# Turning the cross-attention softmax weights on VectorE and through DRAM in a hybrid trunk step

## The chip, the cores and the metric

The kernel runs on one core of a Trainium2 chip. The metric is the time of one execution on the device in microseconds (us); lower is better. PE is TensorE, DVE is VectorE, ACT is ScalarE, POOL is GpSimd and SP is SyncE, whose queue issues most loads. All arithmetic is in float32; matmuls that need the full precision are done in three passes on operands that are split into a high and a low part.

## What is computed

One step of a decoder layer for a prompt group (1024 tokens) and a sample group (8 sequences, one token each). One projection of the normalised input feeds three branches: gated linear attention (GLA), multi-scale causal pooling, and cross-attention into 256 memory tokens (4 heads, head dimension 256). The three are gated, summed and projected out. The change touches the cross-attention of the prompt group:

```python
def cross_attn(q, mk, mv):
    """q: (B,T,H,Dh); mk, mv: (B,M,H,Dh)."""
    s = jnp.einsum('bthd,bmhd->bhtm', q.astype(jnp.float32), mk.astype(jnp.float32)) * (XA_HEAD_DIM ** -0.5)
    p = jax.nn.softmax(s, axis=-1)
    o = jnp.einsum('bhtm,bmhd->bthd', p, mv.astype(jnp.float32))
    return o.astype(q.dtype)

def mixer_layer(...):
    h = rmsnorm(x, norm_gain)
    proj = h @ w_in
    q, k, v, gla_g, a_lr, u, pool_g, xq, xg, merge = jnp.split(proj, split_pts, axis=-1)
    ...
    c = cross_attn(xq.reshape(B, T, XA_HEADS, XA_HEAD_DIM), mem_k, mem_v).reshape(B, T, XA_WIDTH)
    br_x = c * jax.nn.silu(xg)
    branches = jnp.stack([br_gla, br_pool, br_x], axis=2)
    bproj = jnp.einsum('btnw,nwd->btnd', branches, w_branch)
    ...
```

The softmax's weights p have tokens on the partitions (rows); the product with the values contracts over memory tokens, so it needs them with memory tokens on the partitions. The turning between the two is what the change is about.

## The kernel before

**Products.** The input projection is cut into pairs of 128 output columns. Each pair is computed by seven products of a fast block scheme, each product in two halves of 12 matmuls into a PSUM buffer named px (six of these). ACT and DVE read px (names r and c) and hand it on. The weights come by SP into `raw`; DVE and ACT make sums (`ws`) and high and low parts (`a11h`, `s2l` and so on), three products ahead of their use. These products keep PE busy for most of the kernel's first two thirds.

**Work put between.** After each half of a product, `fill` takes more work from a generator, in units of cost that each `yield` states, so that it is spread evenly over the products. First comes `cross_steps`, then the GLA. The matmuls of this work use two more PSUM buffers, named pz.

**The cross stage.** `cross_steps` walks over 16 steps s, one for each head h = s // 4 and each chunk c of 256 tokens. Step s does, in this order: `cross_scores` of s (matmuls, then the maximum nm on DVE, exp into the tile p on ACT, a reciprocal and two scalings on DVE), the split of the queries of s + 1 (`xqsh`, `xq`), the load of the queries of s + 2, once a head the load of the memory's keys and values (`mkv`), then `cross_values` of s - 2 and `cross_weights` of s - 1. `cross_weights` turns p by four transposes on PE (L716) into pz and splits the result into `pTh` (ACT, L222) and `pTl` (DVE, L223). `cross_values` contracts these with the values `mvsh` and `mkv` in 12 matmuls (`mm3`, L241 to L243), ACT copies the result to `xo` (L728), and POOL stores it (`mixsc`, L729). Between these stands the sample group's attention, `cross_sample`: its keys `kc` and its queries `qb` come by SP, DVE multiplies and sums them (L769), PE turns and contracts them (`sc`, `ps`, `pm`, `vc`, L783 to L819). The sample queries reach `qb` by way of a store by POOL (`xqs`, L744).

**Queues.** The orders of PE and SP are those in which the program is written. The order on ACT, DVE and POOL is set by a scheduler when the program is built. A queue runs in order: an instruction that waits holds what stands behind it.

**Buffers.** Most tiles of 128x512 in this stage come from one ring of NR = 14 SBUF buffers (`R`): queries, p, the turned weights, xo, the split keys and values. A new tile takes a buffer whose last tile is done with, and its first writer waits for the last reader of that one. `kc`, `qb` and `vc` come from four buffers of their own (`V`).

Two helpers on which the change rests: `split_in` splits a tile that lies in SBUF, the low part written over the source, and `loaded` takes a ring buffer and issues a load on SP.

Of the kernel before, what the change touches and what calls it, by code (L numbers as in the profile page):

```python
# [18 lines left out]
P = 128  # L19
# [5 lines left out]
NH = 4  # L25
# [8 lines left out]
CT = 256  # L34
# [13 lines left out]
def trunk_kernel(ctx: ExitStack, tc: tile.TileContext,  # L48
# [3 lines left out]
    nc = tc.nc  # L52
# [46 lines left out]
    def PZ():  # L99
        return ps.tile([P, 512], F32, tag="pz", name="pz", bufs=2)  # L100
# [13 lines left out]
    def R(shape, dt=F32, name="r"):  # L114

        return shaped(wk.tile([P, 512], dt, tag="ring", name=name, bufs=NR), shape)
# [20 lines left out]
    ident = cp.tile([P, P], F32, name="ident")  # L137
# [63 lines left out]
    def scratch(n, name, shape):  # L201
        return [dr.tile(list(shape), F32, name=f"{name}{i}") for i in range(n)]

    PAIR = (P, 4, HT)
    xq_scr, v_scr = scratch(NH, "xqs", (NS, 256)), scratch(NH, "vs", (NS, 256))
    acc_scr = [scratch(NK, f"acc{n}_", (P, TT)) for n in range(2)]
    mkv_scr = [scratch(NH, f"mkvs{o}", (P, 2, DV)) for o in range(2)]
    al_scr = scratch(2, "als", (P, HT))
# [19 lines left out]
    def split_r(src, shape, name, scale=None):  # L228
        hi, lo = R(shape, F32R, name + "h"), R(shape, F32R, name + "l")
        split(hi, lo, src, scale)  # L230
        return hi, lo
# [440 lines left out]
    cross = {}  # L672

    def cross_load(h):
        cross["raw", h] = [loaded(mkv_scr[o][h], [2, DV], "mkv") for o in range(2)]
# [16 lines left out]
    def cross_scores(h, c):  # L692
        xh, xl = cross["q", h, c]
        mh, ml = cross["mk", h]
        t = PZ()
        for j in range(2):
            for i in range(2):
                cs = slice(j * P, (j + 1) * P)
                mm3(t[:, j * NM:(j + 1) * NM], xh[:, i, cs], xl[:, i, cs], mh[:, i], ml[:, i], i == 0, i == 1)
        nm = tiny(2, "nm")  # L700
        nc.vector.tensor_reduce(nm, t.rearrange("p (j m) -> p j m", j=2), axis=AX.X, op=ALU.max, negate=True)
        p = R([2, NM], name="p")
        sm = tiny(2, "sm")
        for j in range(2):
            act(p[:, j], t[:, j * NM:(j + 1) * NM], AF.Exp, bias=nm[:, j:j + 1], accum_out=sm[:, j:j + 1])
        nc.vector.reciprocal(sm, sm)
        for j in range(2):
            nc.vector.tensor_scalar(p[:, j], p[:, j], sm[:, j:j + 1], None, op0=ALU.mult)
        cross["p", h, c] = p

    def cross_weights(h, c):
        p = cross["p", h, c]
        t = PZ()
        for a in range(2):
            for j in range(2):
                nc.tensor.transpose(t[:, (2 * a + j) * P:(2 * a + j + 1) * P], p[:, j, a * P:(a + 1) * P], ident)  # L716
        cross["pT", h, c] = split_r(t.rearrange("p (a t) -> p a t", a=2), [2, CT], "pT")

    def cross_values(h, c):
        ph, pl_ = cross["pT", h, c]  # L720
        vh, vl = cross["mv", h]
        g = R([2, CT], name="xo")
        t = PZ()
        for i in range(2):
            cs = slice(i * P, (i + 1) * P)
            for a in range(2):
                mm3(t[:, i * CT:(i + 1) * CT], vh[:, a, cs], vl[:, a, cs], ph[:, a], pl_[:, a], a == 0, a == 1)
        nc.scalar.activation(g, t.rearrange("p (i t) -> p i t", i=2), AF.Copy)  # L728
        nc.gpsimd.dma_start(out=mix_chunk(2, h, c), in_=g)  # L729

# [93 lines left out]
    def cross_steps():  # L824
        def scores(n):
            cross_scores(n // 4, n % 4)

        def memory(n):
            if n % 4 == 0:
                cross_memory(n // 4)  # L830

        def weights(n):
            cross_weights(n // 4, n % 4)

        def values(n):
            cross_values(n // 4, n % 4)

        samples = chain_of(cross_sample(h) for h in range(NH))
        cross_load(0)
        cross_memory(0)  # L840
        cross_fetch(0, 0)
        yield 2
        cross_queries(0, 0)
        cross_fetch(0, 1)
        for s in range(16 + 2):
            if s < 16:
                scores(s)
                yield 3
                if s + 1 < 16:
                    cross_queries(*divmod(s + 1, 4))  # L850
                if s + 2 < 16:
                    cross_fetch(*divmod(s + 2, 4))
            if s % 4 == 2 and s < 14:
                cross_load(s // 4 + 1)
            if s >= 1:
                yield next(samples, 0)
            if 0 <= s - 2:
                values(s - 2)
                yield 1.7
            if s >= 1:  # L860
                yield next(samples, 0)
            if s % 4 == 3 and s < 15:
                memory(s + 1)
                yield 2
            if 0 <= s - 1 < 16:
                weights(s - 1)
                yield 1.7
            for _ in range(3):
                if s >= 1:
                    yield next(samples, 0)  # L870
        yield from samples
# [689 lines left out]
```

## Time and profile before

| | |
|---|---|
| median of 3 runs | 1450.72 us (1450.0 to 1452.0) |
| the profiled execution | 1452.08 us, span of the instructions 1450.2 us |
| granted TensorE clock | 0.999 |
| PE busy | 1421.7 us, 98% of the span |
| DVE, ACT, POOL busy | 906.0, 689.2, 194.9 us (62%, 48%, 13%) |
| traffic | 259.42 MB, mean 179 GB/s |
| the cross stage's steps | softmax of the first step at 125.4 us, of the last at 337.5 us |

A profile is of one execution. "L716" is line 716 of the kernel. A group of instructions is written as line, engine, operation, output <- inputs, count, then busy time, mean time of one in ns, and the idle time of the engine ahead of them with what ended it. A row of waits gives what was waited for, the sum in us, how often, and the longest. The chain that ended last is the path of work followed back from the last instruction. A row with three times such as 569/597/600 gives the shortest, the middle and the longest in ns.

### The profile page before, as it was taken

To read this page: it belongs to the slowest core of one execution; us is meant where nothing else is said; L and a number is where in the kernel's file an instruction comes from. 1 tells how busy PE (TensorE), PEld (TensorE's weight loads), DVE (VectorE), ACT (ScalarE), POOL (GpSimd) and SP (SyncE) were. 2 spreads that over 40 slices of the span, in tenths; PEclk is the share of its full clock that TensorE was granted. 3 is DMA by queue.
4 is the path that set the end of the run, shared out by engine and by line. 5 is a ranking of instruction groups with operands and counts; after the bars stand their busy time and mean duration, and the time that the engine had idled before them with its cause. 6 is when DMAs were issued, how large, how long until landed. Compare 5 with 4: busy or idle time off the path is not lost.

```text
span 1450.2 us, 28260 instructions
## 1 busy us (share of the span) xinstructions
PE 1421.7 (98%) x10753; PEld 1360.2 (94%) x10753; DVE 906.0 (62%) x2107; ACT 689.2 (48%) x1607; POOL 194.9 (13%) x353
## 2 busy tenths in 40 slices
PE   7999999998999999999999999999999999999998
PEld 6899999998899999999999999999999999999876
DVE  6956656666686767766756678785672434544436
ACT  6744435443465666656654445454472333233312
POOL 3112101124341111111111111110010000000000
PEclk9999999999999999999999999999999999999999
DMA  9346665666655453553544455455594677632633
GB/s 335 122 159 207 200 212 184 218 190 164 160 157 183 130 182 126 177 175 125 180 142 152 157 187 182 138 192 168 194 303 147 226 255 236 241 116 71 220 125 117
DMA packets 182739, 259.42 MB, mean 179 GB/s; under 512 B 21436, under 2 KB 131796, under 8 KB 182596
## 3 DMA queue, kind: packets, MB, share of 16 engines
q1 hardware_dynamic: 159900, 183.87, 41.4%
q0 software_dynamic: 22560, 73.56, 14.1%
q8 instruction: 84, 1.38, 0.4%
q14 instruction: 51, 0.42, 0.1%
q10 hardware_dynamic: 144, 0.20, 0.0%
HBM read 180.47 MB, written 77.56 MB: 178 GB/s over the span
## 4 chain that ended last, share of the span: by engine, by line
PE 86%; DMA 5%; DVE 5%; issue 2%; ACT 1%; SPq 0%; DVEq 0%; POOL 0%; ACTq 0%
PE px L241 25%; PE px L242 24%; PE px L243 24%; DMA qb<-xqs 2%; PE pz L243 2%; PE pz L242 2%; PE pz L241 2%; DMA raw<-in_w_in_dram 2%; DVE kc L769 1%; PE pz L403 1%; PE pz L955 1%; PE pz L936 1%; PE pz L809 1%; PE pz L938 1%; DVE ws L304 0%
## 5 line engine op out<-in xcount | busy, mean ns | idle before, releaser
L243 PE MATMUL px<-bh,wbl 128*128 128x384 f32 (+1 forms) x576 | 184.1, 320 | 0.0
L242 PE MATMUL px<-bl,wbh 128*128 128x384 f32 (+1 forms) x576 | 184.1, 320 | 0.0
L241 PE MATMUL px<-bh,wbh 128*128 128x384 f32 (+1 forms) x576 | 183.7, 319 | 0.0
L553 ACT ACTIVATE r<-px 128x258 f32<-128x258 f32 x240 | 90.0, 376 | 45.6 <-PE px L243 45.0
L241 PEld LDWEIGHTS px<-bh,wbh 128*128 128x128 f32 x576 | 108.3, 188 | 0.0
L242 PEld LDWEIGHTS px<-bl,wbh 128*128 128x128 f32 x576 | 108.2, 188 | 0.0
L243 PEld LDWEIGHTS px<-bh,wbl 128*128 128x128 f32 x576 | 108.2, 188 | 0.0
L241 PE MATMUL px<-ot,s1h 128*128 128x258 f32 x320 | 93.9, 293 | 0.0
L241 PE MATMUL px<-ot,s3h 128*128 128x258 f32 x320 | 93.4, 292 | 0.0
L241 PE MATMUL px<-o,s4h 128*128 128x258 f32 x320 | 93.2, 291 | 0.2 <-DVE c L628 0.2
L241 PE MATMUL px<-o,a11h 128*128 128x258 f32 x320 | 92.9, 290 | 0.0
L241 PE MATMUL px<-o,a12h 128*128 128x258 f32 x320 | 92.9, 290 | 0.0
L241 PE MATMUL px<-ot,a22h 128*128 128x258 f32 x320 | 92.9, 290 | 0.0
L241 PE MATMUL px<-ot,s2h 128*128 128x258 f32 x320 | 92.3, 288 | 0.0
L242 PE MATMUL px<-o,a11h 128*128 128x258 f32 x320 | 91.0, 284 | 0.3 <-DVE o L223 0.3
L243 PE MATMUL px<-o,a11l 128*128 128x258 f32 x320 | 90.6, 283 | 0.0
L242 PE MATMUL px<-ot,a22h 128*128 128x258 f32 x320 | 90.5, 283 | 0.0
L242 PE MATMUL px<-ot,s2h 128*128 128x258 f32 x320 | 90.0, 281 | 0.5 <-DVE ot L223 0.5
L243 PE MATMUL px<-ot,s3l 128*128 128x258 f32 x320 | 90.5, 283 | 0.0
L243 PE MATMUL px<-o,a12l 128*128 128x258 f32 x320 | 90.4, 283 | 0.0
L242 PE MATMUL px<-o,a12h 128*128 128x258 f32 x320 | 90.4, 283 | 0.0
L243 PE MATMUL px<-ot,s1l 128*128 128x258 f32 x320 | 90.4, 282 | 0.0
(470 smaller groups left out, 4616.0 us busy)
## 6 DMA issues: line engine op xcount, KB each, us to landing
raw<-in_w_in_dram SPq DMA_DIRECT2D x80, 512.0 KB, 4.0
msc<-c POOLq DMA_DIRECT2D x24, 516.0 KB, 4.3
brsc<-c POOLq DMA_DIRECT2D x24, 516.0 KB, 4.0
sig<-msc SPq DMA_DIRECT2D x24, 516.0 KB, 6.6
mix<-mixsc SPq DMA_DIRECT2D x48, 256.0 KB, 4.5
brr<-brsc SPq DMA_DIRECT2D x48, 256.0 KB, 5.2
wbr<-in_w_branch_dram SPq DMA_DIRECT2D x24, 512.0 KB, 6.1
acc<-sig POOLq DMA_DIRECT2D x16, 516.0 KB, 5.3
```

The costliest lines, as they stand in the source:

```text
L241: nc.tensor.matmul(out, lhsT=lh, rhs=rh, start=start, stop=False, skip_group_check=more)
L242: nc.tensor.matmul(out, lhsT=lh, rhs=rl, start=False, stop=False, skip_group_check=more)
L243: nc.tensor.matmul(out, lhsT=ll, rhs=rh, start=False, stop=stop, skip_group_check=more)
L403: nc.tensor.matmul(t[:, :DV], lhsT=memT[k // 2][:, k % 2, a * P:(a + 1) * P], rhs=raw[k // 2][:, k % 2], start=k == 0, stop=k == NK - 1)
L553: nc.scalar.activation(r, acc[c][:, :QT], AF.Copy)
L769: nc.vector.tensor_tensor_reduce(kc[:, a, :], kc[:, a, :], qb[:, bb, :], scale=1.0, scalar=0.0, op0=ALU.mult, op1=ALU.add, accum_out=sc[:, ...
L809: nc.tensor.matmul(t[32 * j:32 * j + 32, :DV], lhsT=pm[:, a, 4 * i + j, :], rhs=vc[j][:, a, :], start=a == 0, stop=a == 1)
L936: nc.tensor.matmul(t[0:64, 0:P], lhsT=ki[:, 0:64], rhs=qi, start=True, stop=True)
L938: nc.tensor.transpose(t[:, P:2 * P], kt, ident)
L955: nc.tensor.matmul(to, lhsT=kiqi[:, 1, cs], rhs=st, start=False, stop=True)
```

## The change

After the softmax, DVE turns each 32x32 block of p (`STREAM_TRANSPOSE`) into a new tile pt. POOL stores pt to a DRAM scratch in four DMAs, one for each 32 partitions, in pieces of 64 elements. Two steps later SP loads it back into a tile pT with memory tokens on the partitions (`cross_turned`). `cross_weights` splits pT where it lies, and `cross_values` reads the parts in runs of 32 elements, since the columns lie in another order. The weights of a step are split in the iteration two after its softmax (one after it before), and the values are computed in the third (the second before), so the loop has one iteration more. The four PE transposes of each step are gone. Everything else of the program is as it was; lines behind L206 move by one, so that L241 is L242 after, and further by five behind `cross_values`.

```diff
     PAIR = (P, 4, HT)
     xq_scr, v_scr = scratch(NH, "xqs", (NS, 256)), scratch(NH, "vs", (NS, 256))
+    pt_scr = scratch(4 * NH, "pts", (8, 32, 4, 64))
     acc_scr = [scratch(NK, f"acc{n}_", (P, TT)) for n in range(2)]
     mkv_scr = [scratch(NH, f"mkvs{o}", (P, 2, DV)) for o in range(2)]
     al_scr = scratch(2, "als", (P, HT))
@@ -706,15 +707,17 @@
         nc.vector.reciprocal(sm, sm)
         for j in range(2):
             nc.vector.tensor_scalar(p[:, j], p[:, j], sm[:, j:j + 1], None, op0=ALU.mult)
-        cross["p", h, c] = p
+        pt = R([512], name="pt")
+        nc.vector.transpose(pt.rearrange("p (b j c) -> p j b c", j=2, c=32), p.rearrange("p j (b c) -> p j b c", c=32))
+        for q in range(4):
+            nc.gpsimd.dma_start(out=pt_scr[4 * h + c][:, :, q, :].rearrange("b r x -> r b x"),
+                                in_=pt[32 * q:32 * q + 32].rearrange("r (b x) -> r b x", b=8))
 
     def cross_weights(h, c):
-        p = cross["p", h, c]
-        t = PZ()
-        for a in range(2):
-            for j in range(2):
-                nc.tensor.transpose(t[:, (2 * a + j) * P:(2 * a + j + 1) * P], p[:, j, a * P:(a + 1) * P], ident)
-        cross["pT", h, c] = split_r(t.rearrange("p (a t) -> p a t", a=2), [2, CT], "pT")
+        cross["pT", h, c] = split_in(cross["pr", h, c], [2, CT], "pT")
+
+    def cross_turned(h, c):
+        cross["pr", h, c] = loaded(pt_scr[4 * h + c].rearrange("(a b) r q x -> (b r) a (q x)", a=2), [2, CT], "pT")
 
     def cross_values(h, c):
         ph, pl_ = cross["pT", h, c]
@@ -724,7 +727,9 @@
         for i in range(2):
             cs = slice(i * P, (i + 1) * P)
             for a in range(2):
-                mm3(t[:, i * CT:(i + 1) * CT], vh[:, a, cs], vl[:, a, cs], ph[:, a], pl_[:, a], a == 0, a == 1)
+                rh, rl = (x[:, a].rearrange("p (q j c) -> p j q c", q=4, j=2) for x in (ph, pl_))
+                mm3(t[:, i * CT:(i + 1) * CT].rearrange("p (j q c) -> p j q c", j=2, q=4), vh[:, a, cs], vl[:, a, cs],
+                    rh, rl, a == 0, a == 1)
         nc.scalar.activation(g, t.rearrange("p (i t) -> p i t", i=2), AF.Copy)
         nc.gpsimd.dma_start(out=mix_chunk(2, h, c), in_=g)
 
@@ -842,7 +847,7 @@
         yield 2
         cross_queries(0, 0)
         cross_fetch(0, 1)
-        for s in range(16 + 2):
+        for s in range(16 + 3):
             if s < 16:
                 scores(s)
                 yield 3
@@ -852,18 +857,20 @@
                     cross_fetch(*divmod(s + 2, 4))
             if s % 4 == 2 and s < 14:
                 cross_load(s // 4 + 1)
+            if 0 <= s - 2 < 16:
+                cross_turned(*divmod(s - 2, 4))
             if s >= 1:
                 yield next(samples, 0)
-            if 0 <= s - 2:
-                values(s - 2)
+            if 0 <= s - 3:
+                values(s - 3)
                 yield 1.7
             if s >= 1:
                 yield next(samples, 0)
             if s % 4 == 3 and s < 15:
                 memory(s + 1)
                 yield 2
-            if 0 <= s - 1 < 16:
-                weights(s - 1)
+            if 0 <= s - 2 < 16:
+                weights(s - 2)
                 yield 1.7
             for _ in range(3):
                 if s >= 1:
```

By the counts of the program, 64 transposes on PE are left out, and 16 DVE transposes, 64 issues on POOL and 16 loads on SP are added.

**PE, first step whose weights are turned.** Matmuls of a product (px, from the operands ot and s1h) stand around the four transposes; before:

```order
646 L241 MATMUL px<-ot_756,s1h 128x258
647 L242 MATMUL px<-ot_757,s1h 128x258
648 L243 MATMUL px<-ot_756,s1l 128x258
649 L716 MATMUL pz<-ident,p 128x128 x4
650 L241 MATMUL px<-ot_752,s1h 128x258
651 L242 MATMUL px<-ot_753,s1h 128x258
```

After:

```order
646 L242 MATMUL px<-ot_772,s1h 128x258
647 L243 MATMUL px<-ot_773,s1h 128x258
648 L244 MATMUL px<-ot_772,s1l 128x258
649 L242 MATMUL px<-ot_768,s1h 128x258
650 L243 MATMUL px<-ot_769,s1h 128x258
651 L244 MATMUL px<-ot_768,s1l 128x258
```

The transposes are gone and the matmuls of the product follow each other.

**SP, step s = 6** (third step of the second head). The queries (xq), the next head's keys and values (mkv), then the sample group's keys (kc) and queries (qb); raw are weights of the projection. In brackets stand the semaphores that an issue waits on. Before:

```order
89 L662 DMA xq<-xqsc_172 128x2x256 [waits DMASW3_49,DMASW1_49,PE_49]
90 L662 DMA mkv<-mkvs_150 128x512 [waits DMASW7_49,PE_49]
91 L662 DMA mkv<-mkvs_154 128x512 [waits DMAHW3_49,PE_49]
92 L662 DMA kc<-in_cache_mem_k_dram 128x2x256 [waits DMAHW4_49]
93 L662 DMA kc<-in_cache_mem_k_dram 128x2x256 [waits DMAHW6_49,DMAHW5_49,DVE_49]
94 L759 DMA qb<-xqs_125 128x512 [waits DMAHW0_49,DVE_49]
95 L295 DMA raw<-in_w_in_dram 128x4x256 [waits DMAHW7_49,DVE_49]
96 L662 DMA kc<-in_cache_mem_k_dram 128x2x256
97 L662 DMA kc<-in_cache_mem_k_dram 128x2x256 [waits DMAHW4_49,DMAHW1_49,DVE_49]
98 L759 DMA qb<-xqs_125 128x512 [waits DMAHW5_49,DMAHW2_49,DVE_49]
```

After:

```order
93 L663 DMA xq<-xqsc_188 128x2x256 [waits DMAHW5_49,DMASW5_49,PE_49]
94 L663 DMA mkv<-mkvs_166 128x512 [waits DMAHW6_49,PE_49]
95 L663 DMA mkv<-mkvs_170 128x512 [waits DMASW5_49,DMASW6_49,DMASW4_49,DMASW7_49,DMASW3_49,DMAHW7_49,DMASW2_49,DVE_49]
96 L663 DMA pT<-pts_136 128x2x256 [waits DMAHW0_49,PE_49]
97 L663 DMA kc<-in_cache_mem_k_dram 128x2x256 [waits DMAHW1_49]
98 L663 DMA kc<-in_cache_mem_k_dram 128x2x256 [waits DMAHW2_49,DVE_49]
99 L764 DMA qb<-xqs_125 128x512 [waits DMAHW4_49,DMAHW3_49,DVE_49]
100 L663 DMA kc<-in_cache_mem_k_dram 128x2x256
101 L663 DMA kc<-in_cache_mem_k_dram 128x2x256 [waits DMAHW5_49,DMAHW1_49,DVE_49]
102 L764 DMA qb<-xqs_125 128x512 [waits DMAHW6_49,DMAHW2_49,DVE_49]
103 L296 DMA raw<-in_w_in_dram 128x4x256 [waits DMAHW7_49]
```

The load of the turned weights (pT) has come between mkv and kc, and waits on PE. The load of raw stands behind the second qb of these rows and no longer between the two.

**POOL, beginning of the cross stage.** The xqsc and mixsc rows store products and mixed values, smp is a small copy, xqs are the sample group's queries. Before:

```order
66 L587 DMA xqsc_171<-c_1175 128x2x516
67 L568 COPY smp<-c_1427 128x8
68 L587 DMA xqsc_171<-c_1427 128x1032
69 L744 DMA xqs_124<-qn 8x256
70 L568 COPY smp<-c_1541 128x2x4
71 L587 DMA xqsc_172<-c_1541 128x2x516
72 L729 DMA mixsc_0_182<-xo 256x1x256
```

After:

```order
66 L588 DMA xqsc_187<-c_1191 128x2x516
67 L569 COPY smp<-c_1443 128x8
68 L588 DMA xqsc_187<-c_1443 128x1032
69 L713 DMA pts_132<-pt 32x8x64 x4
70 L713 DMA pts_133<-pt 32x8x64 x4
71 L749 DMA xqs_124<-qn 8x256
72 L713 DMA pts_134<-pt 32x8x64 x4
73 L569 COPY smp<-c_1563 128x2x4
74 L588 DMA xqsc_188<-c_1563 128x2x516
```

The stores of the first two steps' turned weights stand ahead of xqs, those of the third behind it.

**ACT, step s = 6.** The copy of the values (xo), the high part of the turned weights (pTh), and the releases of px (r, c) and high parts of weights around them. Before:

```order
186 L728 ACTIVATE xo<-pz 128x512
187 L647 ACTIVATE c_2598<-px 128x258
188 L222 ACTIVATE s3h<-ws 128x512
189 L647 ACTIVATE c_2598<-px 128x258
190 L222 ACTIVATE pTh<-pz 128x512
191 L222 ACTIVATE a11h<-raw 128x512
```

After:

```order
182 L733 ACTIVATE xo<-pz 128x512
183 L223 ACTIVATE s2h<-ws 128x512
184 L554 ACTIVATE r_2632<-px 128x258
185 L223 ACTIVATE pTh<-pT 128x512
186 L223 ACTIVATE s1h<-ws 128x512
187 L648 ACTIVATE c_2652<-px 128x258
```

The split of the weights now reads SBUF (pT) where it read PSUM (pz); it stands three rows behind the copy of the values where it stood four behind it.

## The prediction

> **What bounds the kernel now.** I read the page first (busy time and the chain that ended last), then busy time by stretch, where 100 to 340 us holds the 16 steps of the cross stage, 340 to 380 us its last sample work, and 380 to 1300 us what follows.
>
> ```profile
> PE 1421.7 (98%) x10753; PEld 1360.2 (94%) x10753; DVE 906.0 (62%) x2107; ACT 689.2 (48%) x1607; POOL 194.9 (13%) x353
> PE 86%; DMA 5%; DVE 5%; issue 2%; ACT 1%; SPq 0%; DVEq 0%; POOL 0%; ACTq 0%
> 100.00:340.00 240.00, 236.31 (x1983) 229.15 (x1982) 152.87 (x386) 108.14 (x262) 40.47 (x73) 1.00 0.62 191
> 340.00:380.00 40.00, 32.72 (x272) 29.56 (x271) 18.42 (x50) 12.00 (x27) 16.46 (x27) 1.00 0.68 196
> 380.00:1300.00 920.00, 917.47 (x7160) 899.51 (x7160) 592.57 (x1397) 469.21 (x1118) 111.48 (x186) 1.00 0.55 177
> ```
>
> The columns of the last three rows are length, then PE, PE's weight loads, DVE, ACT and POOL, the granted clock, the share of the DMA engines and GB/s. PE is the bound: from 380 to 1300 us it stands still for 920.00 − 917.47 = 2.5 us. Whatever PE gains before 380 us is therefore carried to the end, since little is there for a shift to fall into. In the two earlier stretches PE stands still for 3.7 and 7.3 us, 11.0 together, and the waits of PE from 100 to 380 us say for what:
>
> ```profile
> PE pz L795 <- DVE ps L790: 2.7, 1, 2.7
> PE pz L242 <- DVE pTl L223: 1.8, 1, 1.8
> PE pz L809 <- DMA vc<-in_cache_mem_v_dram: 1.7, 1, 1.7
> PE pz L241 <- ACT xqsh L225: 1.4, 1, 1.4
> PE pz L243 <- DVE xq L226: 1.3, 2, 1.0
> PE pz L716 <- ACT xo L728: 1.1, 1, 1.1
> PE pz L241 <- DVE pTl L223: 0.8, 1, 0.8
> PE pz L783 <- DVE mkTl L223: 0.2, 1, 0.2
> ```
>
> Three of them hang on the turned weights: 1.8, 1.1 and 0.8, or 3.7 us. So the change can win by PE work that goes, and by these waits, and it can lose by any new wait of PE.
>
> **What goes from PE.** Each of the 16 steps drops four transposes on the identity. Here is the first group in the timeline of PE, then the chain at that group and at a late one, then all groups by line:
>
> ```profile
> 134.44 0.28 PE L243 MATMUL px<-ot,s1l 128*128 128x258 f32 x1
> 134.56 0.60 PE L716 MATMUL pz<-ident,p 128*128 128x128 f32 x4
> 134.92 0.37 PE L241 MATMUL px<-ot,s1h 128*128 128x258 f32 x1
> 135.12 0.28 PE L242 MATMUL px<-ot,s1h 128*128 128x258 f32 x1
> ```
> ```profile
> 134.73 0.44 PE pz L716 x4
> ...
> 316.11 0.44 PE pz L716 x4
> ```
> ```profile
> L716 PE MATMUL pz<-ident,p 128*128 128x128 f32 x64 | 9.7, 273 | 1.1 <-ACT xo L728 1.1
> ```
>
> Matmuls of a product start 0.12 us apart (134.44 to 134.56). From the start of the last one before the group to the start of the second after it are 135.12 − 134.44 = 0.68 us; two of the ordinary distance are 0.24, so the group costs 0.44 us. The chain says the same at both ends of the stage. 16 × 0.44 = 7.0 us of PE. This is the main term.
>
> The last row gives another reading, by the durations: 273 ns each, 64 × 0.273 = 17.5 us. But matmuls overlap: 0.28-us ones start every 0.12 us, so a duration is not a price; I take the starts. [...]
>
> **What is added, and where it lies.** A step's length comes from the softmax's first and last start in this row of the tile p: (337.5 − 125.4) / 15 = 14.1 us.
>
> ```profile
> L75 ACT ACTIVATE p<-pz,nm x32: 462/470/477, 125.4 to 337.5; 128x256 f32<-128x256 f32 x32
> L581 DVE STREAM_TRANSPOSE vt<-c 128x512 f32<-128x512 f32 x10 | 7.0, 703 | 0.1
> 197.80:211.90 14.10, 14.10 (x120) 14.10 (x120) 9.22 (x28) 5.91 (x15) 2.52 (x5) 1.00 0.82 249
> ```
>
> DVE gets 16 transposes of 128x512. The same shape is in the stage already at 703 ns: 16 × 0.70 = 11.2 us, 0.7 of DVE's time in a step. In the step of the third row DVE works 9.22 of 14.10 us, so 4.9 are open, and I cost it at nothing; without that cover it is 11.2 us.
>
> POOL gets four stores a step. Its nearest rows are the 64 stores of vtsc, 64 KB in short runs just like these:
>
> ```profile
> L584 POOL DMA_DIRECT2D vtsc<-vt x64: 649/649/752, 310.5 to 418.4; - x64
> DMA to landing us min/median/max: 2.3/3.2/7.6
> ```
>
> 64 × 0.65 = 42 us, 2.6 a step, while POOL works 2.52 of 14.10 us in the step above: hidden. Landing takes at most 7.6 us, and the load stands two steps (28 us) behind the softmax. What stands behind these stores on POOL are copies of products, the store of the mixed values and that of the sample rows (xqs), put off by up to 2.6 us a step. The first xqs store, for which SP and the sample work wait, now stands behind the stores of step 1; its time now, the end of that step's softmax on ACT and its scaling on DVE:
>
> ```profile
> 134.51 0.53 POOL L744 DMA_DIRECT2D xqs<-qn  x1 [11.68 <-ACT qn L743]
> 131.45 0.47 ACT L75 ACTIVATE p<-pz,nm 128x256 f32<-128x256 f32 x1
> L708 DVE TENSOR_SCALAR p<-p,sm 128x256 f32<-128x256 f32 x32 | 9.9, 352 | 0.5
> ```
>
> From 131.9 DVE needs 2 × 0.35 for the scaling and 0.7 for the transpose, POOL 2.6: 135.9 against 134.5, so 1.4 us late, once. SP's next load of weights comes as much later; none of the old waits of PE is on weights, and I cost it at nothing.
>
> SP gets 16 loads of 256 KB. Nearest: the xq load, same size, 4.3 us to landing; SP itself is held some 0.5 us by the issue.
>
> ```profile
> xq<-xqsc SPq DMA_DIRECT2D x16, 256.0 KB, 4.3
> L222 ACT ACTIVATE pTh<-pz x16: 569/597/600, 135.3 to 362.3; 128x512 fp32r<-128x512 f32 x16
> L222 ACT ACTIVATE vsh<-v x16: 612/618/632, 391.4 to 726.6; 128x512 fp32r<-128x512 f32 x16
> ```
>
> The split reads SBUF where it read PSUM: ACT 618 instead of 597 ns, 0.3 us in all, DVE as before. Traffic is 8.4 MB more (twice 4.2), in a stage whose DMA engines were busy 0.62 of the time: hidden unless a load that is late now gets later.
>
> One SBUF ring buffer more per step is asked of the same 14. That is where new waits come from. In the changed program most turned loads get a buffer whose last reader is long done, or that step's own softmax buffer, released by the DVE transpose. At two of them (the third step of the second and of the third head, s = 6 and s = 10) it is the buffer with the high half of the values of the head just ended, and SP stops until PE's values matmuls of that same step. Step 6 looks like this, SP first, then PE, then one wait of DVE:
>
> ```profile
> 198.41 0.53 SPq L662 DMA_DIRECT2D xq<-xqsc  x1
> 199.03 1.62 SPq L662 DMA_DIRECT2D mkv<-mkvs  x2
> 200.70 4.05 SPq L662 DMA_DIRECT2D kc<-in_cache_mem_k_dram  x2
> 205.06 0.34 SPq L759 DMA_DIRECT2D qb<-xqs  x1
> 209.59 0.37 SPq L295 DMA_DIRECT2D raw<-in_w_in_dram  x1
> ```
> ```profile
> 205.87 0.28 PE L243 MATMUL pz<-pTh,mkv 128*128 128x256 f32 x1
> 214.71 0.69 DVE L304 TENSOR_TENSOR ws<-raw 128x512 f32<-128x512 f32 x1 [1.45 <-DMA raw<-in_w_in_dram]
> ```
>
> SP would stop at about 200.7 (after mkv) until 206.2, when the last of these matmuls is through. So kc and qb, now issued by 205.06, come some 2 us later; the weights (raw), now at 209.59, stand behind one more pair of kc loads and its qb, some 6 us later in all, and DVE had already waited 1.45 us for them. The pT load lands at 206.2 + 4.3 = 210.5; its split stands in ACT's queue three rows behind the copy of the values, about 207.8, so ACT stops there for some 3 us. Cover on PE: six PSUM buffers, each filled by 12 matmuls × 0.12 = 1.44 us, are 8.6 us of work ahead of a reader that stands still; and these weights are needed a step later, some 218.7 (204.6 + 14.1), about 7 us after the split can be done. So: between nothing and 2 × 3 = 6 us for ACT's stops, and as much again for DVE's.
>
> The other way for a late SP to reach PE is DVE at the sample products, of which one row speaks:
>
> ```profile
> DVE kc L769 <- DMA qb<-xqs: 21.1, 10, 4.4
> ```
>
> DVE stands still in its queue for qb already ten times, 21.1 us in all, and PE lost little by it: the whole of PE's waits from 100 to 380 us is 11.0. So 2.1 us of DVE's stopping was covered each time. That speaks for the lower end. For the upper end, each of the 16 steps costs PE as much as the longest wait for the split in the table of waits, 1.8: 29 us.
>
> I take the new waits as equal to the 3.7 us of old ones on the turned weights, because those rows are the same kind of wait (PE behind a split that came late), and the two cancel. Bounds: −3.7 (the old ones go, none come) to +25 (29 − 3.7).
>
> **The values matmuls** read the turned weights in runs of 32 elements instead of one run of 256. No row of the trace shows such a moving operand. The rows of now:
>
> ```profile
> L241 PE MATMUL pz<-pTh,mvsh x64: 277/283/383, 143.7 to 369.1; 128*128 128x256 f32 x64
> ```
>
> Lower bound nothing; upper bound half speed, 192 matmuls × 0.12 = 23 us. I take nothing, since each run is still 32 neighbours long and the number of elements is the same. [...]
>
> **The sum.** −7.0 (transposes) − 3.7 (old waits) + 3.7 (new waits) + 0 (DVE, POOL, SP, ACT, traffic, strides) = −7.0 us. The profiled execution took 1452.1 us (span 1450.2), 1.4 above the median of the runs shown, 1450.7; 1452.1 − 7.0 = 1445.1 for it, and for the median 1450.7 − 7.0 = **1443.7 us**, 0.5% faster. About 0.2% (2.9 us) is what a measurement of this kernel can tell from no change.
>
> **Rivals.** *Taken back* (same): new waits eat the gain. For it: SP's two stops, one ring buffer more per step, and the sample rows' store behind POOL's new ones. Against: SP, ACT and DVE have stops of this size now, and PE hardly shows them. With the upper end of ACT's two stops, 6 us, against 7.0, the time is 1450.7 − 7.0 + 6 = 1449.7, within 0.2%.
>
> *Slower by the sample products.* DVE stops at L769 for a qb that comes after SP's stop or behind the turned loads; PSUM releases and splits stand behind it in DVE's queue. It decides once it takes 7.0 / 16 = 0.44 us from PE in each step. For it: the chain of waits before 400 us already runs through qb; against: the 21.1 us of before that PE did not feel. With 1 us a step the time is 1450.7 − 7.0 + 16 = 1460.
>
> *Slower by the strided read*: half rate at the values matmuls, 1450.7 − 7.0 + 23 = 1467. For it no row; against it only that runs are long.
>
> *More than I reckon*: the durations are the price, 1450.7 − 17.5 = 1433. Against it: the starts and the chain.
>
> **How the numbers follow.** The forecast has 0.57; its own range is 1439.5 (the old waits go too: 1443.7 − 3.7 = 1440.0, and half a microsecond) to 1447.8. Taken back has 0.21, between 1447.8 and 1453.6, the two edges of what can be told. Slower by the sample products 0.14, by the strided read 0.05, more than reckoned 0.03. So faster 0.57 + 0.03 = 0.60, same 0.21, slower 0.19. A range of 1439.5 to 1454.5 takes in 0.02 of the sample products' case and leaves out 0.12 + 0.05 + 0.03 = 0.20.
>
> **What the profile after would show.** Right: no rows of transposes on p; the chain loses its 0.44 pieces; PE's idle time from 100 to 380 us (a little shorter stage) is again near 11 us; the values matmuls last 283 ns and start 0.12 apart; POOL's stores of pt take 0.65 us; turned loads wait longest at two steps of the stage, for PE. Wrong: PE's waits on pT's low half or on ACT's copies grow past 7 us in sum; DVE's waits for qb grow well over 21.1 us and PE's waits with them; values matmuls start 0.2 us apart or more; the store of xqs lands so late that the sample work runs past the stage's end.

## The result: slower by 1.6%

The changed kernel took 1475.6 us (four runs, 1468.5 to 1478.0) against 1451.4 for the one before (four runs); the ratio is 1.016, 95% interval 1.0121 to 1.0199. The forecast was 1443.7 us. The profiled execution took 1477.8 us, 25.7 more than that of before.

Busy time and chain of the page, then the same three stretches as before:

```profile
PE 1428.2 (97%) x10689; PEld 1361.7 (92%) x10689; DVE 914.8 (62%) x2123; ACT 688.5 (47%) x1607; POOL 231.5 (16%) x417
PE 74%; DMA 4%; DVE 3%; issue 1%; ACT 1%; SPq 0%; POOL 0%; DVEq 0%; ACTq 0%
100.00:340.00 240.00, 216.89 (x1725) 204.33 (x1724) 141.52 (x350) 95.96 (x235) 62.65 (x113) 0.96 0.66 202
340.00:380.00 40.00, 35.43 (x276) 34.76 (x275) 28.59 (x79) 14.53 (x35) 19.63 (x33) 0.90 0.69 197
380.00:1300.00 920.00, 914.75 (x7184) 894.71 (x7183) 589.33 (x1396) 468.72 (x1125) 121.72 (x202) 1.00 0.57 181
```

PE has 64 instructions less and yet 6.5 us more busy time, and the granted clock falls to 0.96 and 0.90 in the cross stage, where it was 1.00. From 100 to 340 us PE gets through 1725 instructions instead of 1983. For all comparisons below one stretch holds the stage and its end, 100 to 420 us; here before, then changed:

```profile
100.00:420.00 320.00, 308.38 (x2573) 296.41 (x2572) 206.68 (x527) 146.57 (x360) 74.65 (x129) 1.00 0.62 185
```
```profile
100.00:420.00 320.00, 291.51 (x2323) 275.76 (x2322) 196.49 (x492) 130.56 (x315) 100.49 (x175) 0.96 0.67 199
```

PE stands still for 28.5 us there instead of 11.6. Its waits in that stretch, the largest first:

```profile
PE pz L788 <- DVE sc L774: 10.2, 3, 5.3
PE pz L814 <- DMA vc<-in_cache_mem_v_dram: 5.6, 3, 3.2
PE pz L242 <- ACT xqsh L226: 2.6, 2, 1.4
PE pz L814 <- DVE pm L801: 2.2, 1, 2.2
PE pz L243 <- DVE pT L224: 2.1, 1, 2.1
PE px L242 <- DVE c L629: 1.9, 1, 1.9
```

18.0 us (10.2 + 5.6 + 2.2) are waits for the sample group's attention: its sums (sc), its values (vc), its weights (pm). Only 2.1 are for the turned weights. Here is the longest of these waits in PE's timeline, and the same place by stretches of 2 us, where the clock is the third column from the end:

```profile
164.47 0.28 PE L244 MATMUL px<-ot,s1l 128*128 128x258 f32 x1
170.01 0.63 PE L788 MATMUL pz<-ident,sc 128*8 128x128 f32 x2 [5.26 <-DVE sc L774]
170.29 0.56 PE L242 MATMUL px<-ot,s3h 128*128 128x258 f32 x1
...
170.87 0.42 PE L244 MATMUL px<-ot,s3l 128*128 128x258 f32 x1
171.09 0.42 PE L242 MATMUL px<-ot,s3h 128*128 128x258 f32 x1
171.30 0.42 PE L243 MATMUL px<-ot,s3h 128*128 128x258 f32 x1
```
```profile
166.00:168.00 2.00, 0.00 (x0) 0.00 (x0) 0.00 (x0) 0.00 (x0) 0.00 (x0) 0.84 0.65 103
168.00:170.00 2.00, 0.00 (x0) 0.02 (x1) 1.26 (x7) 0.00 (x0) 0.00 (x0) 0.50 1.02 356
170.00:172.00 2.00, 1.99 (x10) 1.80 (x11) 1.75 (x5) 0.09 (x1) 0.00 (x0) 0.50 0.37 131
172.00:174.00 2.00, 2.00 (x11) 2.00 (x11) 1.75 (x4) 1.86 (x4) 0.00 (x0) 0.50 0.00 0
174.00:176.00 2.00, 2.00 (x18) 2.00 (x17) 1.94 (x6) 0.82 (x3) 0.00 (x0) 0.96 0.00 0
```

PE stops for 5.26 us, the clock falls to half, and for four microseconds after it matmuls start 0.21 us apart instead of 0.12. The clock falls like this at four places (123, 167, 321 and 372 us). So this wait is paid for a second time. The first of the four is not the change's doing: its first added instruction, DVE's transpose at 129.32 us, comes later, and xqs_before, a kernel without the change (below), shows such a fall at 124 us.

The sum of the two profiles: 25.9 us more span are 19.4 of standing still (47.9 against 28.5 in all, 16.9 of it from 100 to 420 us) and 6.5 of busy time. The work taken away makes PE's busy time 6.3 smaller (the run "drop" below: 1415.4 against 1421.7), so some 12.8 us are work on PE that took longer. The clock accounts for about 10 of them: by its column in stretches of 1 us it is at 0.50 for 27.3 us in the stage, PE works in 20.5 of these, and at 0.50 half of that is lost (an estimate; by the starts above, 0.21 us apart instead of 0.12, it is about 9). What the other 2.5 are, the runs do not show; they are nearer 5, since drop itself works 4.7 us at half clock, which costs it 2.4.

### The profile page after: what moved, and what is told of

Its sections match the earlier page's. It is cut to its first block, busy times and chain, and to the rows that moved or that the text cites. A ratio compares the mean times of both kernels' runs of the same rounds, so it can differ in the third digit from the quotient of the medians.

```text
span 1476.1 us, 28345 instructions
## 1 busy us (share of the span) xinstructions
PE 1428.2 (97%) x10689; PEld 1361.7 (92%) x10689; DVE 914.8 (62%) x2123; ACT 688.5 (47%) x1607; POOL 231.5 (16%) x417
## 4 chain that ended last, share of the span: by engine, by line
PE 74%; DMA 4%; DVE 3%; issue 1%; ACT 1%; SPq 0%; POOL 0%; DVEq 0%; ACTq 0%
PE px L242 22%; PE px L243 22%; PE px L244 22%; DMA qb<-xqs 3%; PE pz L242 1%; PE pz L243 1%; PE pz L244 1%; DMA vc<-in_cache_mem_v_dram 1%; PE pz L962 1%; PE pz L943 1%; DVE kc L774 1%; PE pz L814 1%; PE pz L945 1%; PE pz L994 0%; PE pz L906 0%
## 5 line engine op out<-in xcount | busy, mean ns | idle before, releaser
L242 PE MATMUL px<-bh,wbh 128*128 128x384 f32 (+1 forms) x576 | 183.8, 319 | 0.0
L242 PEld LDWEIGHTS px<-bh,wbh 128*128 128x128 f32 x576 | 108.4, 188 | 0.0
L242 PE MATMUL px<-o,s4h 128*128 128x258 f32 x320 | 92.7, 290 | 2.1 <-DVE c L629 2.1
L242 PE MATMUL px<-ot,a22h 128*128 128x258 f32 x320 | 94.1, 294 | 0.0
L242 PE MATMUL px<-ot,s3h 128*128 128x258 f32 x320 | 94.0, 294 | 0.0
L242 PE MATMUL px<-ot,s1h 128*128 128x258 f32 x320 | 93.4, 292 | 0.0
L242 PE MATMUL px<-o,a12h 128*128 128x258 f32 x320 | 93.1, 291 | 0.0
L242 PE MATMUL px<-o,a11h 128*128 128x258 f32 x320 | 92.7, 290 | 0.0
L242 PE MATMUL px<-ot,s2h 128*128 128x258 f32 x320 | 92.5, 289 | 0.0
L244 PE MATMUL px<-ot,a22l 128*128 128x258 f32 x320 | 91.3, 285 | 0.0
L243 PE MATMUL px<-ot,s3h 128*128 128x258 f32 x320 | 90.9, 284 | 0.0
```

Source lines behind the costliest of these rows:

```text
L242: nc.tensor.matmul(out, lhsT=lh, rhs=rh, start=start, stop=False, skip_group_check=more)
L243: nc.tensor.matmul(out, lhsT=lh, rhs=rl, start=False, stop=False, skip_group_check=more)
L244: nc.tensor.matmul(out, lhsT=ll, rhs=rh, start=False, stop=stop, skip_group_check=more)
```

## The experiments

Eighteen kernels ran. The table has the median of each in us, the ratio to the kernel before with its interval, the mean granted clock of the profiled execution, and how long PE stood still from 100 to 420 us in it (320 less its busy time there). In drop, ns_before, ns_after and unread_after work is left out or other data are read, so their outputs are not those of the layer; they serve for the times alone.

The expectations name four theories of the loss. S: the load of the turned weights holds SP's queue, and the sample group's loads behind it come late. D: ACT and DVE are held by the turned path itself. L: PE, with less to do, only runs into sample work that cannot go faster. C, which came later: the sample group's chain (load, sums on DVE, buffer given back, next load) feeds PE at the limit, either as a loop of waits (C-loop) or through its place and traffic in SP's queue (C-queue).

| run | us | ratio (95%) | clock | PE still |
|---|---|---|---|---|
| before (by comparison) | 1450.6 to 1452.1 | | 0.999 | 11.6 |
| changed | 1475.6 | 1.016 (1.012 to 1.020) | 0.990 | 28.5 |
| drop | 1445.4 | 0.995 (0.993 to 0.996) | 0.997 | 10.4 |
| add_t | 1461.0 | 1.006 (1.004 to 1.008) | 0.994 | 15.7 |
| add_ts | 1473.8 | 1.015 (1.013 to 1.017) | 0.992 | 19.5 |
| add | 1481.9 | 1.020 (1.016 to 1.024) | 0.992 | 26.0 |
| xqs | 1465.3 | 1.009 (1.007 to 1.011) | 0.993 | 20.6 |
| xqs_before | 1451.8 | 1.001 (1.000 to 1.002) | 0.996 | 8.9 |
| own | 1509.0 | 1.039 (1.036 to 1.041) | 0.985 | 26.5 |
| late | 1481.7 | 1.021 (1.019 to 1.023) | 0.987 | 24.2 |
| late_xqs | 1477.0 | 1.018 (1.016 to 1.020) | 0.991 | 22.6 |
| poolq_xqs | 1478.0 | 1.019 (1.017 to 1.021) | 0.989 | 29.9 |
| ns_before | 1441.0 | 0.994 (0.992 to 0.995) | 0.999 | 3.4 |
| ns_after | 1439.0 | 0.992 (0.990 to 0.993) | 0.999 | 6.4 |
| unread_after | 1449.6 | 0.999 (0.997 to 1.000) | 0.997 | 12.6 |
| smp | 1476.7 | 1.018 (1.016 to 1.021) | 0.988 | 38.1 |
| smp_before | 1473.9 | 1.017 (1.014 to 1.019) | 0.989 | 25.6 |
| slack_xqs | 1465.4 | 1.011 (1.008 to 1.013) | 0.991 | 21.0 |
| v5_before | 1470.9 | 1.014 (1.012 to 1.015) | 0.994 | 14.7 |
| v5_xqs | 1481.1 | 1.020 (1.018 to 1.022) | 0.989 | 24.2 |

### What the removal is worth, and what each added part costs

The part removed, alone:

```diff
-                nc.tensor.transpose(t[:, (2 * a + j) * P:(2 * a + j + 1) * P], p[:, j, a * P:(a + 1) * P], ident)
+        cross["pT", h, c] = split_r(p, [2, CT], "pT")
```

> The kernel before, with the four PE transposes of each step left out and nothing in their place (the unturned weights are split from SBUF and used). Theory S and rival D: the gain of the removal alone, 1450.7 - 7.0 = 1443.7, within 2 us. Rival L: PE runs into the sample work, waits of PE from 100 to 380 us grow from 11 to 18 us, time 1449 to 1452.

1445.4 us, 6.7 below the kernel before in that comparison. The term of the prediction holds, and rival L falls.

The parts added, one after the other, to a kernel that keeps its PE transposes:

```diff
+        pt = R([512], name="pt")
+        nc.vector.transpose(...)            # add_t
+        nc.gpsimd.dma_start(...)            # four a step: add_ts
+        loaded(pt_scr[4 * h + c]...)        # not used: add
```

> The kernel before, PE transposes kept, with only the 16 DVE transposes added (into a ring buffer, not read). All of transposes, stores and unused loads cost 30 us. Theory S: no transfer is added, so at most the ring's 7th buffer counts: 1451 to 1456. Rival D: DVE has 11.2 us more work in its order, which PE feels where it already waited for DVE: 1455 to 1463.

> The kernel before, PE transposes kept, with the DVE transposes and the 64 stores, but no loads. Theory S: the first xqs store is late (about 10 us, by the run with these stores on ACT), nothing holds SP: 1460 to 1466, and the loads bring the rest up to 1482. Rival D: above what the transposes alone give by less than 5 us.

> The kernel before, PE transposes kept, with the DVE transposes, the stores and the loads of the turned weights added from the same ring and their result not used. Theory S: most of the loss comes with these alone, since SP is held in the same way: 1465 to 1482. Rival D: no instruction of ACT or DVE waits for the loaded weights here, so 1451 to 1456. Rival L: 1450 to 1453, as PE is not faster.

Plus 9.3, 22.1 and 29.8 us, each against its own comparison. So the transposes cost some 9 us, the stores 13 more and the loads 8 more, though DVE, POOL and SP have time for all of it. All three less the gain of the removal are 29.8 − 6.7 = 23.1 us, close to the 24.3 by which the changed kernel is slower. Rival D's number for the transposes and S's for the whole came true; add_ts lies above both ranges, and neither had foreseen that every part costs. In add_t PE stands still only 4.1 us longer in the stage; it also works 13.6 us at half clock there, which is worth 6.8. What add_t does not part is DVE's 11.2 us of work from the ring's seventh buffer a step: SP's other loads now waited for these transposes too,

```profile
SPq L663 <- DVE pt L712: 17.3, 3, 12.7
```

### Three suspects for the way it takes

First the store of the sample queries, moved to ACT in the changed kernel and, as a control, in the one before:

```diff
-        nc.gpsimd.dma_start(out=xq_scr[h], in_=qn[:NS])
+        nc.scalar.dma_start(out=xq_scr[h], in_=qn[:NS])
```

> The changed kernel, with the four stores of the sample queries (xqs) issued by ACT and not by POOL, so that they do not stand behind the stores of pt. Theory S: the first one leaves near 134.5 us as before and not at 138.7, the first stall for the sample sums (5.26 us at 165 to 170 us) shrinks below 2 us and takes its half clock with it, the later ones stay: 1460 to 1470. Rivals D and L: no change, 1470 to 1478.

> The kernel before, with the sample queries' stores issued by ACT. If the 10 us of that move came from the stores of pt standing ahead on POOL, nothing changes here: 1449 to 1452. If ACT is the better queue for them in general, 1440 to 1446.

1465.3 and 1451.8 us: worth 10 us in the changed kernel by the medians (4 by the fastest runs, 1468.5 and 1464.2) and nothing in the other, so this part of the loss is the stores of pt standing ahead on POOL. In the changed kernel POOL's timeline had been

```profile
130.33 2.34 POOL L713 DMA_DIRECT2D pts<-pt  x4 [7.65 <-DVE pt L711]
136.38 2.30 POOL L713 DMA_DIRECT2D pts<-pt  x4 [3.71 <-DVE pt L711]
138.67 0.54 POOL L749 DMA_DIRECT2D xqs<-qn  x1
```

The store of xqs left at 138.67 instead of 134.51. With ACT issuing it the first stall is gone, a later one stays:

```profile
PE pz L788 <- DVE sc L774: 6.1, 2, 4.6
```

Second, the ring buffer for which the load of pT waits on SP. The waits of SP in the changed kernel:

```profile
SPq L663 <- DVE sc L774: 38.8, 12, 5.1
SPq L663 <- DVE pt L711: 30.0, 6, 13.2
...
SPq L663 <- PE pz L244: 16.4, 8, 5.7
```

```diff
+    def TU(shape, dt=F32, name="tu"):
+        return shaped(wk.tile([P, 512], dt, tag="turned", name=name, bufs=2), shape)
-        cross["pr", h, c] = loaded(..., [2, CT], "pT")
+        cross["pr", h, c] = loaded(..., [2, CT], "pT", TU)
-NE = 30
+NE = 29
```

> The changed kernel, with two SBUF buffers of their own for the loaded weights pT (one large buffer of another pool less, 29 instead of 30, to make room). Theory S (supply): the load of pT waits in SP's queue for a ring buffer (30.0 us behind DVE's transposes, 16.4 behind values matmuls), the sample group's loads behind it come late, PE waits for the sample work (18.0 of its 28.4 us of waits from 100 to 420 us), and after a stall of 3 to 5 us the granted clock is 0.50 for some microseconds. Then here the waits of SP before pT go below 10 us, PE's waits for sample work below 8 us, and the time is 1445 to 1455. Rival D (DVE and ACT): ACT and DVE stand still for pT's split whatever SP does (24.1 and 13.3 us); then the time stays above 1465. Rival L (lead): PE, 7 us faster, only runs into sample work that cannot go faster; then the time stays near 1470.

The wait behind DVE's transposes is gone from SP, and PE stands still as before (26.5 us), for the same things:

```profile
PE pz L791 <- DVE sc L777: 10.4, 3, 4.0
PE pz L817 <- DMA vc<-in_cache_mem_v_dram: 5.3, 4, 1.8
```

The 16.4 us behind values matmuls stayed too (19.8), so they were not pT's. As far as the smaller pool leaves this stage as it was, SP's wait for a buffer of pT was not what fed PE late, and this part of theory S falls. The total of 1509 us can't be read as the change's: the smaller pool of large buffers costs later, between 420 and 800 us PE stands still for 16.7 us, against 4.3 in the changed kernel. In poolq_xqs (xqs on ACT, and the load of pT on POOL) nothing of the change is in SP's queue:

> The changed kernel with the sample queries' stores issued by ACT (10 us better alone) and the loads of pT issued by POOL, so that SP's queue has nothing of the change in it. Theory S (SP held by pT): 1445 to 1455. Theory C without SP's part: 1458 to 1466, as with the stores on ACT alone.

1478.0: 12.7 us worse than xqs alone and outside both ranges. PE's waits show what is late now:

```profile
PE pz L243 <- DVE pT L224: 12.9, 4, 4.1
```

Third, ACT's and DVE's waits for the split: 24.1 us of ACT for the load of pT, 13.3 of DVE for ACT. In late the split is written at the beginning of the next iteration:

```diff
+            if 0 <= s - 3 < 16:
+                weights(s - 3)
             if s < 16:
                 scores(s)
...
-                weights(s - 2)
```

> The changed kernel, with the split of the loaded weights written at the beginning of the next iteration and not at the end of its own, so that ACT and DVE come to it half a step later; loads, stores, values and ring as before. Theory S: SP is held as before, time 1470 to 1478. Rival D: ACT's waits for the load of pT fall from 24.1 us to below 6 and DVE's for the split from 13.3 to below 5, DVE releases the weight buffers and sample tiles in time, and the time falls to 1450 to 1460. Rival L fell: the removal alone gained 6.7 us.

> The same with the sample queries' stores issued by ACT, which alone was worth 10 us. Rival D: 1443 to 1452. Theory S: SP's waits before pT remain, 1458 to 1466.

Both became slower, 1481.7 and 1477.0, outside both theories' ranges. ACT's waits for the load did fall, to 6.9 us, but DVE's for ACT's half of the split rose:

```profile
DVE pT L224 <- ACT pTh L223: 24.1, 8, 7.6
```

So one wait took the place of another, and D is not tested cleanly by it.

### The sample group's loads

PE waits for the sample group, whose keys, queries and values come in 80 loads by SP into four buffers: a load waits until DVE (for the values PE) has used a buffer (38.8 and 22.0 us of SP's waits in the changed kernel), then takes 4.3 to 4.9 us to land (the medians of the three there), and DVE waits in its queue for the queries:

```profile
DVE kc L774 <- DMA qb<-xqs: 24.3, 10, 4.6
```

The two ns kernels take these loads out; the sums and products read three tiles loaded once, so nothing waits for the stores of xqs either.

```diff
-            kc = [loaded(ck[...], [2, DV], "kc", V) for bb in range(2)]
-            nc.sync.dma_start(out=qb, in_=xq_scr[h]...)
+            return [fixed["kc"]] * 2, fixed["qb"]
...
+            return [fixed["vc"]] * 4
```

> The kernel before, with the sample group's loads of keys, queries and values taken out: its sums and products (same instructions on DVE and PE) read three tiles that are loaded once. Theory C (chain): PE is fed at the limit by the sample group's chain (buffer released by DVE, load in SP's queue, some 4.5 us to landing, sums on DVE), so the waits of PE for sc, ps, pm and vc go: 1443 to 1449. Rival D: the sample loads don't matter, 1450.

> The changed kernel with the same loads taken out. Theory C: what makes the change slow is that its added work (DVE transposes 9 us alone, stores 13 more, loads 8 more) lengthens that chain; without it the change is worth its 7 us, this run is 5 to 9 us below the one before it and the granted clock is near 1.00. Rival D (DVE, ACT and SP late by the turned path itself): it stays above the run before it by 10 us or more, with PE waiting for products' operands or pT.

The stretch from 100 to 420 us of ns_before, then of ns_after:

```profile
100.00:420.00 320.00, 316.65 (x2660) 306.25 (x2659) 213.65 (x546) 155.19 (x377) 80.13 (x134) 1.00 0.44 126
```
```profile
100.00:420.00 320.00, 313.57 (x2618) 302.21 (x2617) 225.02 (x566) 154.49 (x379) 115.52 (x198) 1.00 0.55 155
```

1441.0 and 1439.0 us. Without the sample group's loads the same change, with all its transposes, stores, loads and ring buffers, costs nothing and gives about 2 us (3.6 in the profiled spans); the clock stays at 1.00 in both. That shows that the loss needs these loads: the added work on DVE, POOL and SP costs nothing by itself. Theory C had expected 5 to 9 us below ns_before; it gives less because PE stands still 3.1 us longer.

Is it the waiting, or these loads' place in SP's queue and their traffic? In unread_after they stay where they are and nobody reads them:

```diff
+            c = w2.rearrange("p (a d) -> p a d", a=2)
+            return [c, c], c
```

> The changed kernel with all loads of the sample group left in SP's queue, but read by nobody: its sums and products read a constant tile, so that neither DVE nor PE waits for kc, qb or vc, and a buffer is free when its load has landed. Theory C-loop (the loss is the waiting for these loads and for the buffers they give back): as with the loads out, 1438 to 1446. Theory C-queue (the loads' traffic and their place in SP's queue among raw, mkv and pT): PE waits for products' weights or pT, 1455 or more.

1449.6 us (ten runs, 1443.4 to 1451.7): between the two ranges, 26 below the changed kernel, but ns_after is 10 lower still. The traffic is all there (212 GB/s in the stage against 199 in the changed kernel), so it is not the main cause. The same edit was not tried on the kernel before; if it gains no more there than ns_before, 9.6 us, at least 16 of the 26 are the change's loss. So both forms of theory C seem to have a part, the waiting the larger one. What is left shows in DVE's waits for the projection's weights, 2.0 us in the kernel before:

```profile
DVE ws L305 <- DMA raw<-in_w_in_dram: 22.2, 6, 6.1
```

Three cures were tried on this chain, and none helped. POOL as the queue of the sample loads (the same edit on both kernels, `nc.gpsimd` for `nc.sync` at kc, qb and vc):

> The changed kernel, with the sample group's loads (kc, qb, vc) issued by POOL and not by SP, so that they no longer stand behind weights, memory and turned weights in SP's queue. Theory C-queue (they come late because of what stands ahead of them on SP): PE's waits for the sample work (18.0 us) fall below 8, clock 0.997 or more, time 1442 to 1452. Theory C-loop (the chain of buffer, load, landing and sums is itself too long for DVE's longer queue): 1462 to 1480, and POOL's stores of pt behind waiting loads may make it worse.

> The kernel before, with the same loads on POOL. Theory C-queue: a little faster, 1444 to 1450. Theory C-loop: no change or slower, 1449 to 1460.

Both are slower than 1470, the second above both its ranges. On POOL the loads stand among stores (in smp one pair of kc behind eight stores of vtsc, 5.27 us), and in one stall of PE of 21.8 us DVE waits twice for a qb, 5.23 and 6.58 us.

```profile
PE pz L788 <- DVE sc L774: 31.4, 3, 21.8
```

More time for the chain (three empty `yield 0` ahead of PE's reading of sc):

> The changed kernel, with xqs stored by ACT and PE's reading of the sample sums (its transposes of sc) written three turns of the interleaving later, about three fifths of a step, so that the chain has more time before PE needs it. Theory C (either form): waits of PE for sc (10.2 us changed, 6.1 with xqs on ACT) go to near 0 and with them the half clock there; more sample work is left to the end, where it waits: 1446 to 1458. If it is not time that the chain lacks: 1462 to 1468, as with xqs on ACT alone.

1465.4, as xqs alone. The waits for sc are gone as both forms expected, but PE waits elsewhere instead:

```profile
PE pz L242 <- ACT p L75: 6.0, 1, 6.0
```

The chain can reach PE also through the queues: in the changed kernel DVE stood 4.62 us at a sample product, until 168.74, and the sums of weights (ws) behind these products in its queue began at 170.47. No run shows that the 6.0 us above came the same way. A fifth buffer for the loads, at the price of one in the ring (5 and 13 for 4 and 14):

> The kernel before with five buffers for the sample group's loads and 13 in the ring (4 and 14). Theory C-loop: one load more can be under way, PE's waits of the end (7.3 us) shrink: 1443 to 1449. If the ring is as tight as the sample buffers: 1450 or more.

> The changed kernel, xqs stored by ACT, with the same 5 and 13 buffers. Theory C-loop: below the 1465 of xqs on ACT alone, 1446 to 1460. If the ring, which the change loads with one buffer more a step, is what is short: 1466 or more.

1470.9 and 1481.1, both slower. They don't decide on the loop, since the smaller ring already costs before the cross stage (the first softmax starts at 132.8 and 130.7 us instead of 125.4 and 125.5). No complete kernel of these beat the one before.

## Why the prediction was wrong

- **The removal, −7.0**: right. drop gained 6.7. The rival by durations (17.5) is refuted by the same run.
- **The strided read, nothing**: right, and its rival falls. The values matmuls last as long as before (medians of 281 and 282 ns, and 282 and 283 before) and start 0.12 us apart:

```profile
155.73 0.28 PE L242 MATMUL pz<-pTh,mvsh 128*128 128x256 f32 x1
155.85 0.28 PE L243 MATMUL pz<-pT,mvsh 128*128 128x256 f32 x1
155.97 0.29 PE L244 MATMUL pz<-pTh,mkv 128*128 128x256 f32 x1
```

No row had shown this ahead of the result; these show it for runs of 32 elements.
- **DVE's transposes, "11.2 us, I cost it at nothing"**: wrong by 9 us (add_t). The cover named was DVE's mean open time in a step. A mean says nothing of a chain that runs through the engine in order; with the sample group's loads out the same transposes cost nothing (ns_after).
- **The first store of xqs, "1.4 us late, once ... I cost it at nothing"**: 4.2 us late, and with the later ones worth 10 us (xqs). POOL's four stores took less than reckoned (2.30 us), but DVE ended the transpose of step 1 at 136.1 and not at 133.3: that step's softmax itself came 2.5 us later (133.93 instead of 131.45), behind the fall of the clock at 123 us.
- **POOL's stores, "hidden", and SP's loads, nothing in the sum**: wrong by 12.8 us (add_ts less add_t) and 7.7 us (add less add_ts). The first includes the late xqs.
- **New waits, "taken as equal to 3.7"**: this is the step that failed. PE stands still 16.9 us longer in the stage. The sum let the new waits be those on the turned weights, of one size with the old. Those came to 2.1 us; 18.0 are for the sample group, where the kernel before has 4.4 (2.7 for ps and 1.7 for vc). The reason given against that was that DVE's 21.1 us of waiting for qb had been covered; how much more this cover would bear, the rows of a wait don't show. The expected stop of SP at s = 6 and s = 10 was the wrong place too: SP's new waits are for DVE's transposes (30.0 us), and own took these away while PE stood still nearly as long in the stage.
- **The clock**: not in the sum at all. Some 10 us are lost in matmuls at half speed, 1.7 of them after the first fall, which is not the change's.
- **The rival that came true** is "slower by the sample products", with 0.14 and 1460. That the loss sits in the sample group is what the runs show; its price left out the clock. The link that it names (DVE held longer for a late qb) is not shown: the prediction's sign for it, waits for qb "well over 21.1 us", came out at 24.3, and in the slower add at 18.8.

What stays open: how the 9 us of add_t part between DVE's time and the ring; how unread_after's remaining 10 us part between traffic and SP's order; and by which link of the chain (DVE's sums, SP's queue, the four buffers) PE is fed late, since each cure moved the waits elsewhere. No run held the clock up while keeping the stalls.

## What to carry to other kernels

Before work is moved to an engine "with time", look for a chain in the stage that already runs through that engine or its queue without slack (here load, sums on DVE, buffer back, next load), and take out that chain's loads from both kernels: this pair of runs tells whether the stage can bear the move. On a kernel that PE bounds, a new stall of PE is to be priced at more than its length, but not by a fixed factor: in the changed kernel 19.4 us of standing still went with 12.8 us of longer work, in add_t 4.4 with 8.3, and in smp, with its one long stall, 26.7 with 2.8. What comes on top of the stall is the work that PE does at half clock: 20.5 us of its time in the stage in the changed kernel. The next section shows what stood ahead of each fall there.

## What was not expected of the hardware

The granted clock goes from 1.00 to 0.50 and back within a stage of one kernel: after the stall of 5.26 us it came back some 4 us after PE had resumed, and matmuls of 258 columns started 0.21 us apart meanwhile. In the profile of the kernel before no 25-us stretch from 25 to 1425 us shows a lower clock; its longest stall there was 2.74 us. The length of a stall does not tell the falls apart: at 122 us both kernels wait 1.39 and 0.28 to 0.29 us, and only the changed one fell to 0.50 there, while its stall of 3.15 us, which ended at 189.29, was followed by no fall.

What stood ahead of the falls can be read from the clock and PE's busy time by short stretches. The four falls of the changed kernel lie at 122.98, 167.35, 320.95 and 372.15 us, 44.37, 153.60 and 51.20 us apart, and the clock stays at 0.50 for 3.41, 6.83, 6.83 and 10.24 us. Within 0.01 us the three distances are 13, 45 and 15 times, and the four lengths one, two, two and three times, 3.413 us (51.20 / 15). So the stretches of that length in step with these falls are the ones to compare. Here are six of them from the changed kernel: the one ahead of the fall at 122.98, the one ahead of that at 167.35, two with the stall of 3.15 us in them, and the ones ahead of the falls at 320.95 and 372.15:

```profile
119.57:122.98 3.41, 1.78 (x13) 1.36 (x11) 2.75 (x5) 2.42 (x5) 0.95 (x2) 1.00 0.66 185
163.94:167.35 3.41, 0.81 (x7) 0.60 (x6) 0.18 (x3) 0.00 (x0) 0.00 (x0) 1.00 0.62 149
184.42:187.83 3.41, 1.72 (x14) 1.10 (x12) 1.58 (x3) 0.66 (x2) 0.00 (x0) 1.00 0.94 244
187.83:191.24 3.41, 1.90 (x14) 0.81 (x15) 0.00 (x0) 0.19 (x1) 0.00 (x0) 1.00 0.11 39
317.54:320.95 3.41, 1.18 (x6) 0.28 (x4) 2.79 (x6) 0.90 (x2) 0.00 (x0) 1.00 0.96 355
368.74:372.15 3.41, 1.50 (x12) 1.51 (x13) 3.41 (x13) 0.23 (x1) 2.64 (x6) 1.00 1.07 367
```

Ahead of the four falls PE stands still for 1.63, 2.60, 2.23 and 1.91 us of 3.41. The stall of 3.15 us lay across an edge, with 1.69 and 1.51 in its two stretches, and no fall came behind either. Of the other stretches at full clock in step with these, from 30 to 1450 us, none has more than 1.48 us. So in this profile much standing still within one stretch goes with a fall behind it, but 1.63 and 1.69 us came out on opposite sides, and what sets the clock is not shown. The changed kernel's own runs spread over 10 us with clocks from 0.989 to 0.993, two to four times the spread of the kernel before (2.3 us in the same comparison, 5 to 6 in the others).
